# A narrow expert's gate in another order, and two raw weight slots turned into halves of split weights

## The chip, the cores and the metric

The kernel runs on one NeuronCore of a Trainium2 chip. TensorE (PE in the profile) multiplies, with weight loads (PEld) running beside the matmuls; VectorE (DVE) and ScalarE (ACT) do elementwise work; GpSimd (POOL) has a little of it in the dense layers; SyncE (SP) issues the loads from HBM. The metric is the device time of one execution in microseconds. The median of three runs of the kernel before is 1550.54 us (1549.85 to 1551.14). One more execution was profiled: it took 1551.01 us, of which 1549.3 us lie between its first and its last instruction.

## The reference, cut to what matters

Two encoder layers on 256 tokens of width 1024, all in float32. What the change touches is the end of the second layer, an expert block that takes most of the time:

```python
def swiglu(xn, w_gu, w_down):
    g, u = jnp.split(xn @ w_gu, 2, axis=-1)
    return (jax.nn.silu(g) * u) @ w_down

def moe_swiglu(xn, router, w_gu, w_down):     # 8 experts of hidden width 3584, each token to 2 of them
    ...
    for e in range(N_EXPERTS):
        out = out + comb[..., e:e + 1] * swiglu(xn, w_gu[e], w_down[e])
    return out
```

Ahead of it come a gated convolution and pooling mixer, two cross-attentions, a dense SwiGLU and a Conformer convolution, with the same kind of weights.

## The kernel before, in words

**Split weights.** TensorE takes its operands in a reduced float32 form (`fp32r`). So that the result keeps float32's precision, each operand is split into two parts: `hi`, a cast of the value, and `lo`, the value less `hi`. A weight chunk is 128 partitions x 2048 float32 (1 MB). `load` (line 143) brings it into a slot of the pool `rawp`, or in the expert block also into one of six `spare` tiles. `split` (line 152) makes its parts in two halves of 1024 columns: for each half a cast on ACT (line 168), and behind it a subtraction on DVE (line 169). The halves lie in the pools `hip` and `lop`, `NPART` slots each. With `NPART = 4` the parts of two chunks exist at a time. A raw slot is free again when its last subtraction is done; a slot of the parts, when TensorE is done with it.

**The expert block** goes through eight positions (`expert`, line 1112), each an expert with the tokens that chose it. In a position j runs over seven strips of 512 hidden columns. A strip has six chunks: two for the gate (`gate_up(j, 0)`), two for the up projection (`gate_up(j, 1)`), two for the down projection of the strip before (`down`). Positions 0, 1, 3, 5 and 7 are wide: up to 128 tokens, three products to a weight (line 211, 212 and 216), twelve matmuls to a chunk. Positions 2, 4 and 6 are narrow: at most 64 tokens. There the tokens' `hi` and `lo` parts stand side by side as 128 columns, so that a chunk takes eight matmuls (line 1108), and PSUM holds the `hi` tokens' results in partitions 0 to 63 and the `lo` tokens' in 64 to 127. The last up chunk of a narrow strip is not split but multiplied as plain float32 (line 1124).

**The gate of a narrow strip** (`gate`, line 1137) runs when both products of the strip are issued. ACT copies the two 64-partition halves of the gate's PSUM tile crosswise into an SBUF tile `esg` (lines 1141 and 1142), DVE adds the PSUM tile to it on 128 partitions (line 1143), so that the sum stands in both halves, and ACT takes the silu (line 1144). DVE then multiplies with the up product into `eh` (line 1148). `to_rows` turns `eh` with TensorE (line 1157) and splits the result on ACT and DVE (lines 1038 and 1039) for the down products.

**The order of the work.** Each engine executes its instructions in one fixed order. In the expert block that order is found by a planner while the kernel is built: it follows the order of the program as a priority and takes what its own model of the engines holds to be ready. `tc.issue_after(x)` makes the instructions of a block come behind `x` where they are on the same engine. SP's loads in the expert block stand in program order; `NAHEAD` of them are issued in the attention ahead of it. `RING` and `kinds` say which load takes a raw slot and which a spare tile, with a period of `NRAW + 6`.

**Raw slots outside the expert block.** In the dense layers all weights pass through the same `NRAW = 11` slots. From the end of the dense SwiGLU to the Conformer's end, six of them hold three pairs of parts split early (`raw_pair`), and one more holds a half of a key weight (`apart`). In the Conformer the weights `pw1` are multiplied unsplit (`product_whole`, line 255), so each holds its raw slot until its product is done.

Of the kernel before, what the change touches and what calls it, by code (L numbers as in the profile page):

```python
# [25 lines left out]
F32 = mybir.dt.float32  # L26
F32R = mybir.dt.float32r
I32 = mybir.dt.int32
AF = mybir.ActivationFunctionType
# [3 lines left out]
P = 128  # L33
# [16 lines left out]
HALF = CAP // 2  # L50
TCKW = dict(schedule_with_timeline_sim=True)
NCKW = dict(dynamic_dma_scratch_size=512)
NRAW = 11
NPART = 4
RING = "rrrrrrrrsssssrrrrrs"
P2_POOL = (0, 2, 4, 6)
NWARM = 10
NAHEAD = 13
G_TAPS = 4 * (11, 12)


# [20 lines left out]
def _build(ctx, tc, io, cap):  # L82
    nc = tc.nc
    PSUM = bass.MemoryType.PSUM
    const = ctx.enter_context(tc.tile_pool(name="const", bufs=1))
    rawp = ctx.enter_context(tc.tile_pool(name="rawp", bufs=NRAW))
    hip = ctx.enter_context(tc.tile_pool(name="hip", bufs=NPART))
    lop = ctx.enter_context(tc.tile_pool(name="lop", bufs=NPART))
    big = ctx.enter_context(tc.tile_pool(name="big", bufs=10))
    work = ctx.enter_context(tc.tile_pool(name="work", bufs=2))  # L90
    w2b, w1b = 4, 5
# [6 lines left out]
    V, S, G, PE = nc.vector, nc.scalar, nc.gpsimd, nc.tensor  # L98

    def f32(ap):  # L100
        return ap.bitcast(F32)
# [4 lines left out]
    def acc_tile(name="acc"):  # L106
        return psA.tile([P, 512], F32, tag="acc", name=name)
# [4 lines left out]
    def tr_tile(name="tr", dt=F32):  # L112
        return psT.tile([P, 512], dt, tag="tr", name=name)
# [29 lines left out]
    def load(ap, n=CH, pieces=1, spare=False):  # L143
        raw = big_tile("spare") if spare else rawp.tile([P, CH], F32, tag="raw", name="raw")
        for i in range(pieces):
            sl = slice(i * n // pieces, (i + 1) * n // pieces)
            nc.sync.dma_start(raw[:, sl], ap[:, sl])
        return raw

    done = []  # L150
# [535 lines left out]
    half = KF // 2  # L686
    ps = None
    for m in range(KD):
# [6 lines left out]
        for hf in range(2):  # L695
# [4 lines left out]
            for kk in range(half):  # L700
                k = hf * half + kk
                h, sl = hid[k // 8], slice((k % 8) * T, (k % 8 + 1) * T)
# [218 lines left out]
    ahead = deque()  # L921
    kinds = list(RING)

    def fetch():
        n, (ap, pieces) = next(source)
        ahead.append(load(ap, pieces=pieces, spare=kinds[n] == "s"))
        kinds.append(kinds[-(NRAW + 6)])

    for _ in range(NAHEAD):
        fetch()  # L930
# [103 lines left out]
    def side_by_side(dst, src):  # L1034

        v = dst.rearrange("p (k s n) -> p k s n", s=2, n=HALF)
        src = src.rearrange("p (k n) -> p k n", n=HALF)
        S.copy(v[:, :, 0, :], src)
        V.tensor_sub(v[:, :, 1, :], src, f32(v[:, :, 0, :]))
# [48 lines left out]
    def out_tiles():  # L1088
        return [psE.tile([P, 512], F32, tag="py", name=f"py{n}") for n in range(2)]
# [5 lines left out]
    def whole_chunk():  # L1095
        if not ahead:
            fetch()
        return ahead.popleft()

    def chunk(pieces=2):  # L1100
        return split(whole_chunk(), pieces=pieces)

    def narrow(ps, xs, ws, first, last):

        n = len(xs)
        for part in range(2):
            for i, (x, w) in enumerate(zip(xs, ws)):
                ins = PE.matmul(ps, x, w[part], start=first and i == part == 0,  # L1108
                                stop=last and part == 1 and i == n - 1)
        return ins  # L1110

    def expert(e, g, following):
        nonlocal fn
        py = out_tiles()
        two = e in NARROW

        def gate_up(j, gu):
            pz = acc_tile("gu")
            for kh in range(2):
                xs = [xg[:, k * P:(k + 1) * P] for k in range(kh * 4, kh * 4 + 4)]  # L1120
                if two and gu == kh == 1:
                    w = whole_chunk()
                    for kk in range(4):
                        PE.matmul(pz, f32(xs[kk]), w[:, kk * 512:(kk + 1) * 512],  # L1124
                                  start=False, stop=kk == 3)
                    continue
                w = chunk()
                ws = [w(kk * 512, (kk + 1) * 512) for kk in range(4)]
                if two:
                    narrow(pz, xs, ws, kh == 0, kh == 1)  # L1130
                    continue
                moving(pz, [(xg[:, k * P:(k + 1) * P], xg[:, D + k * P:D + (k + 1) * P])
                            for k in range(kh * 4, kh * 4 + 4)],
                       ws, kh == 0, kh == 1)
            return pz

        def gate(pg, pu):
            sg = work.tile([P, 512], F32, tag="w2", name="esg", bufs=w2b)
            if two:

                S.copy(sg[:HALF], pg[HALF:])
                S.copy(sg[HALF:], pg[:HALF])
                V.tensor_add(sg, sg, pg)
                S.activation(sg, sg, AF.Silu, scale=g.cw[:, 1:2])
            else:
                S.activation(sg, pg, AF.Silu, scale=g.cw[:, 1:2])
            h = work.tile([P, 512], F32, tag="w2", name="eh", bufs=w2b)
            V.scalar_tensor_tensor(h, pu, g.cw[:, 1:2], sg, op0=ALU.mult, op1=ALU.mult)
            return h

        def to_rows(j, h):
            pt = tr_tile("ht")
            o = (j % 2) * D
            if two:

                for i in range(4):
                    PE.matmul(pt[:, i * HALF:(i + 1) * HALF], h[:, i * P:(i + 1) * P], both,
                              start=True, stop=True)
                return side_by_side(ht[:, o:o + 512], pt[:, :4 * HALF])
            for i in range(4):  # L1160
                PE.transpose(pt[:, i * P:(i + 1) * P], h[:, i * P:(i + 1) * P], ident)
            S.copy(ht[:, o:o + 512], pt)
            V.tensor_sub(ht[:, o + 512:o + D], pt, f32(ht[:, o:o + 512]))

        def down(j, n):
            w = chunk(4 if e == NE - 1 and j == 6 else 2)
            o = (j % 2) * D
            if two:
                return narrow(py[n], [ht[:, o + f * P:o + (f + 1) * P] for f in range(4)],
                              [w(f * 512, (f + 1) * 512) for f in range(4)], j == 0, j == 6)  # L1170
            return moving(py[n],
                   [(ht[:, o + f * P:o + (f + 1) * P], ht[:, o + 512 + f * P:o + 512 + (f + 1) * P])
                    for f in range(4)],
                   [w(f * 512, (f + 1) * 512) for f in range(4)], j == 0, j == 6)

        def weighted(n):
            src = py[n]
            hi, lo = (work.tile([P, 512], F32R, tag="w2", name=name, bufs=w2b) for name in ("yh", "yl"))
            S.activation(hi, src, AF.Copy, scale=g.cw[:, 0:1])
            done[:] = [V.scalar_tensor_tensor(lo, src, g.cw[:, 0:1], f32(hi),  # L1180
                                              op0=ALU.mult, op1=ALU.subtract)]
            return hi, lo

        def scatter(n, y, tile=tr_tile):
            for t in range(2):
                pz = tile("so")
                PE.matmul(pz, g.oT[:, t * P:(t + 1) * P], y[0], start=True, stop=False)
                PE.matmul(pz, g.oT[:, t * P:(t + 1) * P], y[1], start=False, stop=True)
                a = acc[:, t * D + n * 512:t * D + (n + 1) * 512]
                V.tensor_add(a, a, pz)  # L1190

        h = None
        for j in range(7):
            pg = gate_up(j, 0)
            if j:
                to_rows(j - 1, h)
            pu = gate_up(j, 1)
            h = gate(pg, pu)
            if j:
                down(j - 1, 0)  # L1200
                if j == 6:
                    to_rows(6, h)
                down(j - 1, 1)
            if following is not None and j in (3, 5):
                following.step(j)
        if following is not None:
            following.rows()
        else:
            fn = big_tile("fn")
            nc.sync.dma_start(fn[:, :D], io["final_norm"].to_broadcast([P, D]))  # L1210
        down(6, 0)
        y = weighted(0)
        last = down(6, 1)
        if following is not None:
            scatter(0, y)
            scatter(1, weighted(1))
        else:
            y1 = weighted(1)
            with tc.issue_after(last.ins):
                scatter(0, y)  # L1220
            scatter(1, y1, acc_tile)

    g = Gather(0)
# [88 lines left out]
    for e in range(NE):  # L1312
        following = Gather(e + 1) if e + 1 < NE else None
        expert(e, g, following)
        g = following
# [174 lines left out]
```

## Time and profile before

| | us |
|---|---|
| median of three runs | 1550.54 |
| the profiled execution | 1551.01 |
| its span, first to last instruction | 1549.3 |
| expert block, first gate matmul to the last down matmul | 594.1 to 1533.5 |
| one strip of a wide position | 16.8 |
| one strip of a narrow position | 13.0 to 15.6 |

Busy time of an engine is the union of its instructions. The end of a matmul is modelled, and matmuls overlap in the pipeline, so PE can look busy where the next matmul comes late; weight loads show the pace as well. An idle stretch of an engine carries the name of what ended it. The profile's share of DMA is the mean busy share of the 16 DMA engines.

### The profile page before, as it was taken

The numbers are of one execution on the slowest core, as the hardware profiler recorded it, in microseconds if no ns is written. First come the engines' busy times: TensorE is split into PE (matmuls) and PEld (weight loads), VectorE is DVE, ScalarE is ACT, GpSimd is POOL, SyncE is SP. The second block draws the span as 40 slices with busy tenths as digits, with TensorE's granted clock in tenths as the row PEclk, the third lists the DMA queues.
The fourth block names the chain that finished last, engine by engine and source line by source line (L and its number), as shares of the span: only waits on it lengthen the run. The fifth ranks groups of instructions, "written<-read, shape, count | busy, mean of one in ns | idle before, by whom it ended". The sixth has DMA issues, their size and how long they took to land.

```text
span 1549.3 us, 23644 instructions
## 1 busy us (share of the span) xinstructions
PE 1513.3 (98%) x8558; PEld 1295.2 (84%) x8558; DVE 1298.1 (84%) x1730; ACT 1052.1 (68%) x1381; POOL 149.0 (10%) x230
## 2 busy tenths in 40 slices
PE   8899999999999999999999999999999999999996
PEld 8899999999998998888888778888667888667885
DVE  7866677776898868989989989889889888889897
ACT  6454554455575657777777877777777777777775
POOL 4710000001294210000000000000000000000000
PEclk9999999999999999999999999999999999999998
DMA  9654454436545566999999999999999999999940
GB/s 371 266 181 159 146 176 166 138 98 226 210 137 222 186 254 217 378 370 335 373 374 336 402 422 407 382 364 341 406 395 378 370 362 341 403 398 371 387 177 30
DMA packets 65214, 451.43 MB, mean 291 GB/s; under 512 B 7360, under 2 KB 7488, under 8 KB 12480
## 3 DMA queue, kind: packets, MB, share of 16 engines
q1 hardware_dynamic: 65088, 449.83, 76.7%
q8 instruction: 69, 1.13, 0.3%
q14 instruction: 57, 0.47, 0.1%
HBM read 448.75 MB, written 1.05 MB: 290 GB/s over the span
## 4 chain that ended last, share of the span: by engine, by line
PE 81%; DVE 9%; POOL 3%; issue 3%; ACT 2%; DMA 1%; SPq 0%; DVEq 0%; POOLq 0%; ACTq 0%
PE gu L211 8%; PE gu L212 8%; PE gu L216 8%; PE acc L205 7%; PE acc L204 7%; PE acc L203 7%; DVE lo L169 7%; PE gu L1124 5%; PE gu L1108 4%; PE py L211 4%; PE py L216 4%; PE py L212 4%; PE py L1108 3%; POOL part L764 2%; PE gx L1027 1%
## 5 line engine op out<-in xcount | busy, mean ns | idle before, releaser
L169 DVE TENSOR_TENSOR lo<-raw,hi 128x1024 fp32r<-128x1024 f32 (+3 forms) x573 | 671.0, 1208 | 120.1 <-ACT hi L168 110.4
L168 ACT CAST hi<-raw 128x1024 fp32r<-128x1024 f32 (+3 forms) x573 | 565.6, 1031 | 213.5 <-PE acc L204 92.0
L169 DVE TENSOR_TENSOR lo<-spare,hi 128x1024 fp32r<-128x1024 f32 (+1 forms) x226 | 261.4, 1203 | 24.6 <-ACT hi L168 20.5
L168 ACT CAST hi<-spare 128x1024 fp32r<-128x1024 f32 (+1 forms) x226 | 221.5, 1036 | 23.6 <-PE gu L212 11.9
L211 PE MATMUL gu<-hi,xg 128*128 128x512 f32 x560 | 218.8, 391 | 0.0
L212 PE MATMUL gu<-hi,xg 128*128 128x512 f32 x560 | 218.4, 390 | 0.0
L216 PE MATMUL gu<-lo,xg 128*128 128x512 f32 x560 | 154.2, 391 | 0.7 <-DVE lo L169 0.7
L216 PEld LDWEIGHTS gu<-lo,xg 128*128 128x128 f32 x560 | 104.7, 188 | 23.9 <-DVE lo L169 1.9
L211 PEld LDWEIGHTS gu<-hi,xg 128*128 128x128 f32 x560 | 105.1, 188 | 22.2 <-ACT hi L168 0.2
L212 PEld LDWEIGHTS gu<-hi,xg 128*128 128x128 f32 x560 | 105.1, 188 | 21.8
L211 PE MATMUL py<-hi,ht 128*128 128x512 f32 x280 | 111.1, 398 | 0.0
L212 PE MATMUL py<-hi,ht 128*128 128x512 f32 x280 | 109.3, 390 | 0.0
L205 PE MATMUL acc<-a2h,lo 128*128 128x256 f32 x336 | 95.2, 283 | 0.0
L204 PE MATMUL acc<-a2l,hi 128*128 128x256 f32 x336 | 95.2, 283 | 0.0
L203 PE MATMUL acc<-a2h,hi 128*128 128x256 f32 x336 | 95.1, 283 | 0.0
L1386 POOL TENSOR_TENSOR fo<-accum,fn 128x512 f32<-128x512 f32 x2 | 2.5, 1268 | 949.1 <-DVE accum L1190 949.1
L1108 PE MATMUL gu<-lo,xg 128*128 128x512 f32 x252 | 80.3, 411 | 8.0 <-DVE lo L169 8.0
L216 PE MATMUL py<-lo,ht 128*128 128x512 f32 x280 | 84.0, 395 | 0.0
L1108 PE MATMUL gu<-hi,xg 128*128 128x512 f32 x252 | 71.2, 396 | 0.0
L1108 PEld LDWEIGHTS gu<-lo,xg 128*128 128x128 f32 x252 | 43.4, 188 | 31.6 <-DVE lo L169 25.2
L203 PEld LDWEIGHTS acc<-a2h,hi 128*128 128x128 f32 x336 | 64.5, 192 | 0.0
L205 PEld LDWEIGHTS acc<-a2h,lo 128*128 128x128 f32 x336 | 64.5, 192 | 0.0
(421 smaller groups left out, 3176.9 us busy)
## 6 DMA issues: line engine op xcount, KB each, us to landing
raw<-in_moe_gu SPq DMA_DIRECT2D x139, 1024.0 KB, 7.1
spare<-in_moe_gu SPq DMA_DIRECT2D x85, 1024.0 KB, 7.2
raw<-in_moe_down SPq DMA_DIRECT2D x78, 1024.0 KB, 7.3
spare<-in_moe_down SPq DMA_DIRECT2D x32, 1024.0 KB, 7.0
raw<-in_ffn_gu SPq DMA_DIRECT2D x22, 1024.0 KB, 4.8
raw<-in_pw SPq DMA_DIRECT2D x12, 1024.0 KB, 4.9
raw<-in_ffn_down SPq DMA_DIRECT2D x16, 704.0 KB, 4.1
raw<-in_wk SPq DMA_DIRECT2D x8, 1024.0 KB, 7.1
```

What stands on the lines that cost most here:

```text
L168: done[:] = (S.copy(hi[:, i:i + step], raw[:, a + i:a + i + step]), V.tensor_sub(lo[:, i:i + step], raw[:, a + i:a + i + step], f32(hi[:, ...
L169: V.tensor_sub(lo[:, i:i + step], raw[:, a + i:a + i + step], f32(hi[:, i:i + step])))
L203: PE.matmul(ps, a[0], b[0], start=first, stop=False)
L204: PE.matmul(ps, a[0], b[1], start=False, stop=False)
L205: PE.matmul(ps, a[1], b[0], start=False, stop=last)
L211: PE.matmul(ps, a[0], b[0], start=first and i == 0, stop=False)
L212: PE.matmul(ps, a[1], b[0], start=False, stop=False)
L216: ins = PE.matmul(ps, a[0], b[1], start=False, stop=last and i == n - 1)
L764: G.tensor_add(part, part, prod)
L1027: PE.matmul(px[:, kk * P:(kk + 1) * P], xt[:, t * D + d0:t * D + d0 + P], oh[:, t, :], start=t == 0, stop=t == 1)
L1108: ins = PE.matmul(ps, x, w[part], start=first and i == part == 0, stop=last and part == 1 and i == n - 1)
L1124: PE.matmul(pz, f32(xs[kk]), w[:, kk * 512:(kk + 1) * 512], start=False, stop=kk == 3)
```

## The change

The pools: `NRAW` goes from 11 to 9, `NPART` from 4 to 6, in the same SBUF space; `RING` and `NAHEAD` follow the shorter ring. The gate in narrow positions: one copy instead of two, the addition on 64 partitions, both written in the program right behind the gate's products, ahead of `to_rows` and the up products. The silu is taken twice from the 64-partition sum, first into the upper half and then in place, and these instructions come behind the last cast on ACT of the up products (`done[0]`). In wide positions the gate stays as it is.

```diff
-NRAW = 11
-NPART = 4
-RING = "rrrrrrrrsssssrrrrrs"
+NRAW = 9
+NPART = 6
+RING = "rrrrrrrsssssrrrrs"
...
-NAHEAD = 13
+NAHEAD = 12
...
-        def gate(pg, pu):
-            sg = work.tile([P, 512], F32, tag="w2", name="esg", bufs=w2b)
+        def gate(pg, pu, sg):
             if two:
 
-                S.copy(sg[:HALF], pg[HALF:])
-                S.copy(sg[HALF:], pg[:HALF])
-                V.tensor_add(sg, sg, pg)
-                S.activation(sg, sg, AF.Silu, scale=g.cw[:, 1:2])
+                for half in (sg[HALF:], sg[:HALF]):
+                    S.activation(half, sg[:HALF], AF.Silu, scale=g.cw[:HALF, 1:2])
             else:
+                sg = work.tile([P, 512], F32, tag="w2", name="esg", bufs=w2b)
                 S.activation(sg, pg, AF.Silu, scale=g.cw[:, 1:2])
...
             pg = gate_up(j, 0)
+            sg = None
+            if two:
+                sg = work.tile([P, 512], F32, tag="w2", name="esg", bufs=w2b)
+                S.copy(sg[:HALF], pg[HALF:])
+                V.tensor_add(sg[:HALF], sg[:HALF], pg[:HALF])
             if j:
                 to_rows(j - 1, h)
             pu = gate_up(j, 1)
-            h = gate(pg, pu)
+            with tc.issue_after(done[0].ins) if two else nullcontext():
+                h = gate(pg, pu, sg)
```

## Rows read from the trace of the kernel before

**Rows 1.** The page's busy times: us, share of the span, instructions.

```profile
PE 1513.3 (98%) x8558; PEld 1295.2 (84%) x8558; DVE 1298.1 (84%) x1730; ACT 1052.1 (68%) x1381; POOL 149.0 (10%) x230
```

**Rows 2.** Stretches of narrow positions 2, 4, 6: length, busy times, PEclk, DMA share, GB/s.

```profile
838.00:940.00 102.00, 101.15 (x439) 74.39 (x437) 93.83 (x97) 84.37 (x102) 0.00 (x0) 1.00 0.98 395
1063.00:1177.00 114.00, 109.85 (x454) 76.04 (x454) 98.14 (x105) 85.26 (x104) 0.00 (x0) 1.00 0.97 384
1300.00:1412.00 112.00, 107.85 (x447) 74.42 (x446) 96.88 (x100) 83.76 (x103) 0.00 (x0) 1.00 0.98 383
```

**Rows 3.** The same view cut at starts of the narrow gate's product; last row wide.

```profile
862.64:916.55 53.91, 53.91 (x229) 39.81 (x228) 49.29 (x51) 46.67 (x56) 0.00 (x0) 1.00 1.00 416
890.13:903.09 12.96, 12.96 (x55) 9.53 (x54) 12.96 (x13) 10.99 (x13) 0.00 (x0) 1.00 1.01 424
916.55:932.11 15.56, 14.71 (x57) 9.54 (x56) 13.12 (x14) 12.01 (x16) 0.00 (x0) 1.00 1.01 422
1088.93:1167.07 78.14, 73.99 (x287) 48.35 (x286) 65.77 (x67) 59.20 (x73) 0.00 (x0) 1.00 1.00 401
1323.86:1402.00 78.14, 73.99 (x287) 48.36 (x286) 65.77 (x66) 59.21 (x73) 0.00 (x0) 1.00 1.00 401
1002.17:1018.96 16.79, 16.79 (x77) 13.91 (x76) 15.06 (x14) 12.65 (x15) 0.00 (x0) 1.00 0.98 375
```

**Rows 4.** The chain that ended last, in a stretch of position 4, by line.

```profile
by line: DVE lo L169 48.3%; PE gu L1124 23.5%; issue 17.4%; PE gu L1108 4.5%; PE py L1108 4.2%; DVE ht L1039 2.5%; DVEq L169 0.6%; DVE eh L1148 0.2%; PE ht L1157 0.2%
```

**Rows 5.** Timeline of ACT in position 4: start, length, instruction, idle before it.

```profile
1122.55 5.79 ACT L168 CAST hi<-raw 128x1024 fp32r<-128x1024 f32 x6
1129.91 0.59 ACT L1141 COPY esg<-gu 64x512 f32<-64x512 f32 x1 [1.57 <-PE gu L1108]
...
1131.99 0.72 ACT L1144 ACTIVATE esg<-esg,cw 128x512 f32<-128x512 f32 x1 [0.90 <-DVE esg L1143]
1132.62 1.98 ACT L168 CAST hi<-raw 128x1024 fp32r<-128x1024 f32 x2
```

**Rows 6.** Timeline of DVE in the same strip.

```profile
1131.27 0.69 DVE L1143 TENSOR_TENSOR esg<-esg,gu 128x512 f32<-128x512 f32 x1
1133.68 1.23 DVE L169 TENSOR_TENSOR lo<-raw,hi 128x1024 fp32r<-128x1024 f32 x1 [1.72 <-ACT hi L168]
1135.63 0.75 DVE L1148 SCALAR_TENSOR_TENSOR eh<-gu,cw,esg 128x512 f32<-128x512 f32 x1 [0.72 <-PE gu L1124]
```

**Rows 7.** Timeline of all engines in a strip of position 2.

```profile
898.69 0.58 ACT L1142 COPY esg<-gu 64x512 f32<-64x512 f32 x1
899.25 3.59 PE L1124 MATMUL gu<-raw,xg 128*128 128x512 f32 x8
899.29 1.99 ACT L168 CAST hi<-spare 128x1024 fp32r<-128x1024 f32 x2
900.23 0.68 DVE L1143 TENSOR_TENSOR esg<-esg,gu 128x512 f32<-128x512 f32 x1
900.82 2.36 DVE L169 TENSOR_TENSOR lo<-spare,hi 128x1024 fp32r<-128x1024 f32 x2
901.19 0.72 ACT L1144 ACTIVATE esg<-esg,cw 128x512 f32<-128x512 f32 x1
```

**Rows 8.** Costliest groups of ACT, shapes apart: busy us, mean ns, idle before.

```profile
L1162 ACT CAST ht<-ht 128x512 fp32r<-128x512 f32 x35 | 20.5, 584 | 34.4 <-PE ht L1161 34.4
```

**Rows 9.** SP's timeline in position 4: its last four loads.

```profile
1124.24 7.48 SPq L147 DMA_DIRECT2D raw<-in_moe_down  x4
```

**Rows 10.** SP's waits, 360 to 520 us: us in total, times, longest.

```profile
SPq L147 <- PE acc L255: 45.1, 8, 6.9
```

**Rows 11.** Loads by destination: count, size, median us from issue to landing.

```profile
raw<-in_moe_down SPq DMA_DIRECT2D x78, 1024.0 KB, 7.3
raw<-in_pw SPq DMA_DIRECT2D x12, 1024.0 KB, 4.9
```

**Rows 12.** Timeline of PE in the Conformer: one product of an unsplit weight.

```profile
434.20 7.07 PE L255 MATMUL acc<-a,raw 128*128 128x256 f32 x32
```

## The prediction

> **What bounds the kernel now.** I read the page's busy times first. PE is busy 98% of the span, DVE 84%, ACT 68% [rows 1]: by these the kernel is TensorE's, and little is left. The change aims at the three narrow positions, so the next view is busy time by stretch. In positions 2, 4 and 6 PE sits idle 0.85, 4.15 and 4.15 us [rows 2], 9.15 us together (102.00 less 101.15, and so on).
>
> That is not the whole loss. Cut into strips, from one `eh` to the next, a narrow strip takes 12.96 us at best, with PE and DVE both busy throughout. Four strips of position 2 take 53.91 us, 13.48 each. The last strip of position 2 takes 15.56, and the five whole strips in each of positions 4 and 6 take 78.14, 15.63 each [rows 3]. The work is the same: PEld is busy 9.53 us in the 12.96 us strip and 48.35/5 = 9.67 in the slow ones. So the slow strips lose about 2.7 us, of which the matmuls' busy time shows 0.8 (78.14 less 73.99, over 5).
>
> By the Trainium skill ("Perfetto Trace Analysis", Identifying the Most-Contended Engine) matmul busy time is a poor measure of the room left, because matmuls are pipelined, and weight-load time a better one. By the first measure the change could win 9 us at most; by the second some 30 (2.7 in 11 strips), and the equal weight loads in strips of 13 and 15.6 us bear the second out.
>
> Where do the 2.7 us go? The chain through position 4 is 48% subtractions and 24% the plain float32 chunk [rows 4], so they alternate. The timelines show how. ACT casts the up halves, waits 1.57 us for the gate's products, copies twice, waits 0.90 us for DVE's addition, takes the silu, and only then casts for the down chunk, at 1132.62 [rows 5]: 1129.91 + 0.59 + 0.58 + 0.90 + 0.72 with small overlaps. DVE, done with the addition at 1131.96, has nothing to subtract until 1133.68. It gets one half in, and then `eh`, next in its queue, waits 0.72 us for the float32 chunk's end [rows 6]. DVE thus idles 2.44 us beside PE's chunk, and afterwards PE waits for DVE. In position 2 the plan has two casts between copies and silu, two subtractions before `eh`, and no such hole [rows 7]. A slow strip is an order of the queues, not a lack of an engine: DVE works 13.1 us in either kind [rows 3].
>
> **The change part by part.**
>
> *Two part slots more each (4 to 6).* ACT may be three chunks ahead of PE instead of two. At the gate's copies the slots hold the second gate chunk and the up chunk; now the down chunk fits beside them. ACT's 1.57 us wait can be two casts (1.98 us the pair [rows 5]), and DVE then has two subtractions (2.36 us [rows 7]) to do in the 1.72 us in which it had none. By itself this fills the hole if the planner uses it.
>
> *Copy and addition behind the gate's products, silu behind the last up cast.* ACT has one copy (0.59) fewer and one silu more. A silu on 64 partitions has no row. From below it is the 64-partition copy, 0.58; from above the 128-partition silu, 0.72 [rows 5, 7]. I take 0.72, since a 64-partition copy of 512 columns takes as long as a 128-partition cast of 512 (0.59 against 584 ns [rows 5, 8]): partitions don't count. The addition on 64 partitions stays at 0.69 for the same reason (halved, 0.34, at best). So ACT gains 0 to 0.14 us a strip, 2.9 us in 21 strips at most. What hides it is ACT's free time: 59.20/5 = 11.84 us of work in a strip of 13.5 [rows 3]; without that cover it is 2.9 us. The copies' wait for the gate's products remains; queued behind it on ACT are casts, for which DVE waits, and behind those PE. That is the danger of the earlier place, priced among the rivals. The gate's PSUM tile comes free earlier and `esg` is held longer (one of four slots); neither is waited for in these rows, so 0, to either side a us or two at the three position changes.
>
> *Two raw slots fewer (ring 17 to 15), one load fewer ahead.* In position 4 SP issues the last four loads from 1124.24, in 7.48 us; 7.3 us later the last has landed, at about 1139 [rows 9, 11]. TensorE needs those chunks after the last `eh` at 1167.07 [rows 3], 28 us later; at 2.6 us a chunk (15.6 over 6) some 10 chunks wait landed. With 15 slots 8 or 9 wait. A strip of 13.5 us wants six chunks, 6.29 MB, or 466 GB/s, and the best stretch gave 424 [rows 3]: 14.8 us, so 1.3 us a strip and 9 us a position, or 3.5 chunks, come out of the stock. A wide strip of 16.79 us gives back 2 us. The stock lasts; cost 0. If the cover were gone, narrow strips would take 14.8.
>
> *The same slots in the dense layers.* Six raw slots hold early parts and one `apart`; 9 - 7 = 2 are left for `pw1`, where there were 4. SP already waits for these products, 45.1 us in eight waits [rows 10], harmlessly, since loads run ahead. With two slots a load is issued as a product ends, and its 4.9 us [rows 11] fit beside the next product's 7.07 [rows 12]: cost 0. More part slots let casts run ahead in the dense layers too; PE is fed there, 0, bounded by a few us either way.
>
> The Trainium skill (the same page, Optimization Strategy) takes a gap that repeats for a sign of too few buffers. By that rule the four part slots alone are at fault and the gate's edit is idle. Position 2 differs: its fast strips ran with the same four. The sum is the same by either, since both are changed.
>
> **The sum.** All slow strips go to the mean of position 2's fast four, 13.5 us. Positions 4 and 6: 78.14 - 67.5 = 10.64 each, 21.3. The last strip of position 2: 15.56 - 13.5 = 2.1. Together 23.4, against the profiled execution's 1551.0 (span 1549.3 and 1.7 around it): 1527.6. The three runs' median, 1550.5, is half a us lower, so I say 1527.5. At best, all strips at 12.96: (78.14 - 64.8) x 2 + (69.47 - 64.8) = 31.4, or 1519.6; a few us at the position changes could come on top. What is late next is DVE: 13.1 us of work in a strip of 13.5, so no more is to be had without taking work from it.
>
> **Rivals.**
>
> *Half of it.* The planner keeps one of the two holes: the silu again directly behind the addition, as [rows 5] show, or `eh` too early [rows 6]. For it: order alone made 13 or 15.6 in this trace, and the planner is the same. Against: six slots allow ACT and DVE to work ahead. A strip of 14.5: 78.14 - 72.5 = 5.6 twice, and 1: 12.3, so 1538.5.
>
> *No gain.* The copy, now ahead of the up casts in the program, stands ahead of them on ACT and waits for the gate's end with casts behind it. Copy 0.59, addition 0.69, subtraction 1.2 then pass before PE's first up `lo`, where four `hi` matmuls cover about 1 us (12.96 us over 55 of them [rows 3], 0.24 each): 1.5 us, and more for the second half. The hole has only moved: strips stay near 15.6, 1550.5. Against: with more slots the up casts can be done before the gate's products are. It decides by whether casts of the up chunk stand before the copy.
>
> *Slower: the Conformer starves.* If a third long-held raw tile leaves `pw1` one slot, each of six products waits for its load: 6 x 4.9 = 29 us, against the 23 won: 1557. For it: SP waits for these products already. Against: the count leaves two, and 4.9 is under 7.07. It decides from the point where one slot is left between two products.
>
> **How the numbers follow.** The forecast 56% (its own range 1516 to 1536), half of it 17%, no gain 13%, slower 12%, and 2% a time below 1516, won at the position changes or in the dense layers besides. 1514 to 1552 leaves out the slower case and a sliver. About 0.2%, 3.1 us, is what a measurement of this kernel can tell from no change. Forecast, half and the rest below it make 0.75 faster; of no gain most is the same, 0.11; slower 0.14, with the part of no gain that comes out above.
>
> **What would show it.** Strips from `eh` to `eh` in positions 4 and 6 of 13.0 to 14, like position 2's; DVE's 1.72 us wait for a cast behind the addition gone, casts between addition and silu; the chain there mostly subtractions, no longer alternating with the float32 chunk; wide strips still 16.8; products of line 255 still 7 us apart. Wrong would be: strips at 15.6 with ACT waiting for the gate's products ahead of up casts, PE idle behind `pw1` loads, or narrow strips of 14.8 with DMA at its limit.

## The result and the profile after

The changed kernel takes 1563.5 us (median of 4 runs, 1561.7 to 1564.0), where the kernel before takes 1550.5 (1549.9 to 1551.1). The ratio is 1.0082, 95% interval 1.0065 to 1.0099: slower by 0.8%. The forecast was 1527.5, faster, and the range ended at 1552. It was wrong in sign.

The profiled execution took 1561.7 us, its span 1560.0, 10.7 more than before. First the page's busy times, to be held against [rows 1].

```profile
PE 1518.6 (97%) x8558; PEld 1294.1 (83%) x8558; DVE 1298.2 (83%) x1730; ACT 1049.7 (67%) x1381; POOL 151.1 (10%) x230
```

The number of instructions is the same, and so, within 3 us, is the work of DVE and ACT; the kernel waits more. Next, stretches from `eh` to `eh` (length, then busy PE, PEld, DVE, ACT, POOL, granted clock, DMA share, GB/s): five strips of position 2, its first and its last, a wide strip, five strips of positions 4 and 6.

```profile
868.67:942.43 73.76, 71.41 (x287) 48.87 (x286) 60.84 (x64) 56.03 (x69) 0.00 (x0) 1.00 1.00 416
868.67:881.97 13.30, 13.30 (x58) 9.79 (x57) 11.44 (x14) 10.78 (x15) 0.00 (x0) 1.00 0.97 407
926.87:942.43 15.56, 14.70 (x57) 9.53 (x56) 13.09 (x15) 11.89 (x15) 0.00 (x0) 1.00 1.00 411
1012.48:1029.27 16.79, 16.79 (x77) 13.90 (x76) 15.06 (x14) 12.65 (x15) 0.00 (x0) 1.00 0.97 368
1099.33:1177.40 78.07, 73.95 (x287) 48.33 (x286) 65.56 (x67) 59.62 (x72) 0.00 (x0) 1.00 0.99 400
1334.70:1412.80 78.10, 73.75 (x286) 47.99 (x285) 65.59 (x68) 59.64 (x72) 0.00 (x0) 1.00 0.99 397
```

Positions 4 and 6 stand where they stood: 78.07 and 78.10 us against 78.14 [rows 3]. Nothing of the forecast's gain came. Position 2 got slower: its strips are 13.3, 14.2, 14.8, 15.9 and 15.6 us, where they were 14.0, 13.4, 13.0, 13.5 and 15.6. That is 4.3 us of the 10.7. Before it, the first `eh` of the expert block starts at 614.0, not 608.5: 5.5 us come from the dense layers. The rest, 0.9 us, is what gains and losses in the wide positions and at the changes between positions leave.

**A narrow strip after.** ACT in position 4, to be read against [rows 5] (start, length, instruction, idle before it and what ended it):

```profile
1132.90 3.90 ACT L168 CAST hi<-spare 128x1024 fp32r<-128x1024 f32 x4
1136.69 2.00 ACT L168 CAST hi<-raw 128x1024 fp32r<-128x1024 f32 x2
1140.26 0.58 ACT L1196 COPY esg<-gu 64x512 f32<-64x512 f32 x1 [1.57 <-PE gu L1108]
1142.34 1.47 ACT L1141 ACTIVATE esg<-esg,cw 64x512 f32<-64x512 f32 x2 [1.50 <-DVE esg L1197]
1143.72 3.87 ACT L168 CAST hi<-raw 128x1024 fp32r<-128x1024 f32 x4
```

DVE beside it, against [rows 6]:

```profile
1139.36 2.35 DVE L169 TENSOR_TENSOR lo<-raw,hi 128x1024 fp32r<-128x1024 f32 x2
1141.63 0.67 DVE L1197 TENSOR_TENSOR esg<-esg,gu 64x512 f32<-64x512 f32 x1
1144.77 1.23 DVE L169 TENSOR_TENSOR lo<-raw,hi 128x1024 fp32r<-128x1024 f32 x1 [2.47 <-ACT hi L168]
1145.97 0.75 DVE L1146 SCALAR_TENSOR_TENSOR eh<-gu,cw,esg 128x512 f32<-128x512 f32 x1
```

ACT still casts six halves and then waits 1.57 us at the copy, though there are six part slots. DVE's hole behind the addition was 1.72 us, and `eh` then waited 0.72: together 2.44. Now the hole is 2.47 and `eh` waits for nothing. It is the two silus, 1.47, and one cast, 1.0, in a row: ACT may not cast for the down chunk until the silus are done, and they wait for an addition that stands on DVE behind the up chunk's subtractions. DVE's 13.1 us of work and 2.47 are the strip of 15.6. The waits in those five strips say it too (us in total, times, longest); before, the first of these lines had 8.6, 5, 1.7 and the silu's wait for the addition 4.5, 5, 0.9:

```profile
DVE lo L169 <- ACT hi L168: 14.9, 6, 2.5
ACT esg L1141 <- DVE esg L1197: 7.4, 5, 1.5
```

**The dense layers.** SP's loads around the Conformer, in the kernel before:

```profile
387.28 0.33 SPq L147 DMA_DIRECT2D raw<-in_wv  x1
391.24 0.33 SPq L147 DMA_DIRECT2D raw<-in_wk  x1
405.75 2.76 SPq L147 DMA_DIRECT2D raw<-in_pw  x3
```

and after:

```profile
400.58 0.33 SPq L147 DMA_DIRECT2D raw<-in_wv  x1
404.00 0.33 SPq L147 DMA_DIRECT2D raw<-in_wk  x1
410.91 3.15 SPq L147 DMA_DIRECT2D raw<-in_pw  x2
```

Product 0 of `pw1` ends at 403.8. Its slot goes at 404.00 to the fourth `wk` chunk, and the third product's load (product 2) must wait for product 1's slot, free at 410.91. With 4.9 us of flight it lands at 415.8, where product 2 begins; before, product 2 began at 413.0 although everything ahead of it was 2.3 us later then. PE's timeline after shows the wait, with products 2, 3 and 4 behind it:

```profile
415.76 23.49 PE L255 MATMUL acc<-a,raw 128*128 128x256 f32 x96 [4.88 <-DMA raw<-in_pw]
```

The wait is not the whole cost. These are product 2 before, and then, after, a part of product 2, all of it, and product 3 (columns as above):

```profile
413.05:419.95 6.90, 6.90 (x33) 6.08 (x32) 6.47 (x17) 5.14 (x12) 5.20 (x8) 1.00 0.68 262
```

```profile
416.60:419.50 2.90, 2.90 (x8) 2.27 (x8) 2.90 (x9) 0.51 (x1) 2.59 (x5) 0.50 0.41 170
415.76:425.27 9.51, 9.51 (x33) 7.98 (x33) 9.51 (x25) 1.19 (x3) 4.49 (x7) 0.73 0.21 87
425.27:432.18 6.91, 6.91 (x34) 6.08 (x33) 6.55 (x17) 5.66 (x13) 5.16 (x8) 1.00 0.46 152
```

While PE waits, its granted clock falls to 0.50, the lower of its two levels (1.2 GHz against 2.4), and product 2 takes 9.51 us instead of 6.90. So the late load costs 4.9 us of waiting and 2.6 us of slower matmuls. Less the 2.3 us by which this execution was ahead (0.5 us in `raw9_only` below), that is the 5.3 us by which product 3 starts late, and nearly all of the expert block's 5.5.

### The profile page after: what moved, and what is told of

The parts are those of the page before. It is cut to its first block, busy times and chain, and to the rows that moved or that the text cites. A ratio compares the mean times of both kernels' runs of the same rounds, so it can differ in the third digit from the quotient of the medians.

```text
span 1560.0 us, 23466 instructions
## 1 busy us (share of the span) xinstructions
PE 1518.6 (97%) x8558; PEld 1294.1 (83%) x8558; DVE 1298.2 (83%) x1730; ACT 1049.7 (67%) x1381; POOL 151.1 (10%) x230
## 4 chain that ended last, share of the span: by engine, by line
PE 75%; DVE 13%; issue 5%; ACT 3%; POOL 2%; DMA 1%; SPq 0%; DVEq 0%; POOLq 0%; ACTq 0%
DVE lo L169 8%; PE gu L216 8%; PE gu L211 8%; PE gu L212 8%; PE acc L204 7%; PE acc L205 7%; PE acc L203 7%; PE py L211 4%; PE py L216 4%; PE py L212 4%; PE gu L1124 2%; PE gu L1108 2%; PE py L1108 2%; DVE cacc L770 2%; PE acc L255 2%
## 5 line engine op out<-in xcount | busy, mean ns | idle before, releaser
L169 DVE TENSOR_TENSOR lo<-raw,hi 128x1024 fp32r<-128x1024 f32 (+3 forms) x557 | 645.2, 1196 | 109.9 <-ACT hi L168 102.8
L168 ACT CAST hi<-raw 128x1024 fp32r<-128x1024 f32 (+3 forms) x557 | 542.9, 1024 | 194.2 <-PE acc L204 77.5
L169 DVE TENSOR_TENSOR lo<-spare,hi 128x1024 fp32r<-128x1024 f32 x242 | 283.5, 1219 | 38.8 <-ACT hi L168 36.6
L168 ACT CAST hi<-spare 128x1024 fp32r<-128x1024 f32 x242 | 238.7, 1049 | 24.8 <-PE gu L212 15.9
L216 PE MATMUL py<-lo,ht 128*128 128x512 f32 x280 | 79.8, 391 | 0.0
L764 POOL TENSOR_TENSOR part<-part,prod 128x256 f32<-128x256 f32 x84 | 61.1, 743 | 47.7 <-ACT prod L763 43.6
```

What stands on the lines that cost most here:

```text
L168: done[:] = (S.copy(hi[:, i:i + step], raw[:, a + i:a + i + step]), V.tensor_sub(lo[:, i:i + step], raw[:, a + i:a + i + step], f32(hi[:, ...
L169: V.tensor_sub(lo[:, i:i + step], raw[:, a + i:a + i + step], f32(hi[:, i:i + step])))
L216: ins = PE.matmul(ps, a[0], b[1], start=False, stop=last and i == n - 1)
L764: G.tensor_add(part, part, prod)
```

## The experiments

Each ratio is to the kernel before (medians 1550.3 to 1550.6).

**The two parts of the change, each alone.** `gate_only` has the new gate and the old pools (`NRAW = 11`, `NPART = 4`, old `RING`, `NAHEAD = 13`); `pools_only` has the new pools and the old gate.

> Only the gate's edit, with the pools of before (11 raw slots, 4 part slots, ring 17, 13 loads ahead). Theory: the time lost comes from the pools and the narrow strips are set by the order of the queues, which the gate's edit leaves as it was (silu directly behind the addition, casts for the down chunk behind the silu). So third pw1 product at 413 us +-1 as before, strips of positions 4 and 6 still 15.5 to 15.7, position 2 from first to last eh 77 to 80 us as before: 1549 to 1553 us. Rival, the gate's edit itself costs: 1556 us or more, with position 2 at 81 us or longer.

> Only the pools' edit (9 raw slots, 6 part slots, ring 15, 12 loads ahead), with the gate of before. Theory: it has the whole loss. Third pw1 product waits some 5 us for its load (start near 415 instead of 413, the fourth 5 us late), position 2 is 3 to 5 us longer because its order settles earlier into the slow one, positions 4 and 6 stay at 15.6 a strip though six part slots are there: 1559 to 1565 us. Rival, six part slots help and the new gate spoils it: strips of 13 to 14.5 us and 1540 us or less.

Measured: `gate_only` 1551.5, ratio 1.0006 (0.9996 to 1.0015): nothing. `pools_only` 1562.7, ratio 1.0075 (1.0059 to 1.0092): the whole loss, with the third product at 417.5 instead of near 415. Position 4 shows that neither part shortens a strip (five strips of `gate_only`, then of `pools_only`):

```profile
1088.80:1166.90 78.10, 73.96 (x287) 48.31 (x286) 65.56 (x67) 59.65 (x72) 0.00 (x0) 1.00 1.00 400
```

```profile
1101.20:1179.40 78.20, 74.14 (x289) 48.40 (x288) 65.85 (x67) 59.27 (x73) 0.00 (x0) 1.00 1.00 401
```

**Fewer raw slots, or more part slots?** `raw9_only` is the kernel before with nine raw slots and four part slots.

```diff
-NRAW = 11
+NRAW = 9
-RING = "rrrrrrrrsssssrrrrrs"
+RING = "rrrrrrrsssssrrrrs"
-NAHEAD = 13
+NAHEAD = 12
```

> The kernel before with nine raw slots, ring 15 and 12 loads ahead, part slots still four, old gate: the two slots' memory stays unused. Theory (raw slots alone make the dense loss and position 2's): third pw1 product 4 to 6 us late, position 2 from first to last eh 79 to 82 us, strips of 4 and 6 at 15.6: 1556 to 1563 us. Rival (six part slots let casts run ahead on ACT and DVE and delay the dense layers): 1549 to 1553 us.

Measured: 1560.8, ratio 1.0067 (1.005 to 1.0084). The first `eh` starts at 614.9, 6.4 late; position 2's five strips take 72.4 us against 69.5 and turn slow one strip earlier than before; positions 4 and 6 are unchanged. Taking two raw slots away, with the ring and the loads ahead that follow from it, is the loss, and two part slots more give nothing for it.

**The silu behind the down chunk's casts.** In narrow strips the first down chunk is split ahead of the gate's end, so that `done[0]` is its last cast and not the up chunk's. `late_after` does this to the changed kernel, `late_gate_only` to `gate_only`. `chunk()` splits the next chunk of the load order; `down` takes it as `wd`.

```diff
...
+            wd = chunk() if two and j else None
             with tc.issue_after(done[0].ins) if two else nullcontext():
                 h = gate(pg, pu, sg)
...
-                down(j - 1, 0)
+                down(j - 1, 0, wd)
```

> The changed kernel, with one edit: in narrow positions the first down chunk is split ahead of the gate's second half, so that the silu stands behind the casts of that chunk instead of behind those of the up chunk. Theory: the narrow strip is a loop of DVE (13.1 us), silu (1.5) and one cast (1.0), and it opens when two casts stand between copy and silu: strips of 13.0 to 13.8 us in positions 4 and 6, DVE's wait of 2.47 us gone, 10 us less in each of the two and 3 to 5 less in position 2; the Conformer's loss stays: 1536 to 1543 us. Rival, something else holds the strip at 15.6 (loads, or PE's chain through the plain float32 chunk): 1558 to 1564 us.

> The same edit (silu behind the casts of the first down chunk) and the changed gate, but with the pools of before. Theory: four part slots are enough, as in position 2 of before: strips of 13.0 to 13.8 in positions 4 and 6, no loss in the Conformer: 1526 to 1533 us. Rival, four part slots are too few, since the down chunk's casts must wait for the slots of the second gate chunk: strips of 14.5 to 15.6 and 1540 to 1552 us.

Measured: 1556.5 (ratio 1.0039, 1.0024 to 1.0053) and 1545.6 (0.9965, 0.9953 to 0.9978). They gain 7.0 us on the changed kernel and 5.9 on `gate_only`, at most a third of what was expected: strips fell to 15.2, not to 13.5. For `late_gate_only` that lies in its rival's range (four part slots too few), but with six part slots `late_after` has the same strips, so the slots are not what holds them. In `late_gate_only` DVE's hole behind the addition is gone, and a new wait stands at `eh`:

```profile
1129.18 0.67 DVE L1197 TENSOR_TENSOR esg<-esg,gu 64x512 f32<-64x512 f32 x1
1129.78 2.35 DVE L169 TENSOR_TENSOR lo<-raw,hi 128x1024 fp32r<-128x1024 f32 x2
1133.59 0.75 DVE L1146 SCALAR_TENSOR_TENSOR eh<-gu,cw,esg 128x512 f32<-128x512 f32 x1 [1.47 <-PE gu L1124]
```

`eh` waits for the up product's float32 chunk on PE, and behind it stand the second down chunk's subtractions, which PE wants next. The loop was the order of two queues, and one of the two had been mended.

**`eh` behind the second down chunk's subtractions too.** `eh_behind_before_pools` has four part slots and eleven raw ones, `eh_behind_six_parts` six and nine. `product_of` is the last line of the old `gate`, the product `eh`; `done[1]` is the last subtraction on DVE.

```diff
...
-            wd = chunk() if two and j else None
+            wd, we = (chunk() if two and j else None), None
             with tc.issue_after(done[0].ins) if two else nullcontext():
-                h = gate(pg, pu, sg)
+                sg = gate(pg, pu, sg)
+            if two and j:
+                we = chunk()
+            with tc.issue_after(done[1].ins) if two else nullcontext():
+                h = product_of(pu, sg)
...
-                down(j - 1, 1)
+                down(j - 1, 1, we)
```

> As late_gate_only (pools of before, changed gate, silu behind the casts of the first down chunk), and besides the second down chunk is split ahead of the gate's product eh, which stands behind that chunk's last subtraction on DVE. What is left in late_gate_only's strip of 15.2 us is DVE's wait of 1.5 us at eh for the float32 chunk, and 0.5 for a cast behind the turned rows. Theory (the strip is a loop through DVE's queue; four subtractions instead of two fit beside the float32 chunk): strips of 13.0 to 14.0 in positions 4 and 6, 8 us less in each of the two, 1526 to 1534 us. Rival (four part slots bind: the second down chunk's casts wait for the slots of the up chunk and all later ones come late): strips of 14.5 or more, 1540 us or more.

> The same edit on the changed kernel's pools (9 raw, 6 part slots). Theory: strips of 13.0 to 13.8, and position 2 too, where four slots keep a mixed order; Conformer's loss of 5 to 7 us and position 1 to 2 stay: 1533 to 1541 us. Rival (the strips' 15 us come from elsewhere): 1553 us or more.

Measured: 1531.9 (ratio 0.988, 0.9863 to 0.9896), which beats both kernels, and 1540.9 (0.994, 0.9923 to 0.9956). In position 4 the strips are 13.5, 14.1, 13.5, 14.7 and 14.3 us with four part slots, and the same with six. The five together, first `eh_behind_before_pools`, then `eh_behind_six_parts`:

```profile
1089.05:1159.17 70.12, 69.02 (x288) 49.81 (x287) 65.42 (x68) 59.94 (x72) 0.00 (x0) 1.00 1.01 418
```

```profile
1096.60:1166.80 70.20, 69.08 (x288) 49.88 (x287) 65.52 (x68) 59.73 (x72) 0.00 (x0) 1.00 1.01 417
```

So the strip was an order, as the prediction read it, and two part slots more have no part in it. The Trainium skill ("Perfetto Trace Analysis", Optimization Strategy) says that a repeating gap can mean too few buffers; here six part slots left it at 15.6 us, and the order alone closed most of it with four.

**Which part of the gate's edit is needed?** `whole_gate_moved` is `eh_behind_before_pools` with the gate's old arithmetic in the new place: two copies, the addition and one silu on 128 partitions.

```diff
                 S.copy(sg[:HALF], pg[HALF:])
-                V.tensor_add(sg[:HALF], sg[:HALF], pg[:HALF])
+                S.copy(sg[HALF:], pg[:HALF])
+                V.tensor_add(sg, sg, pg)
...
-                for half in (sg[HALF:], sg[:HALF]):
-                    S.activation(half, sg[:HALF], AF.Silu, scale=g.cw[:HALF, 1:2])
+                S.activation(sg, sg, AF.Silu, scale=g.cw[:, 1:2])
```

> Like eh_behind_before_pools (1531.9 us: eleven raw slots, four part slots, silu behind the first down chunk's casts, eh behind the second's subtractions), but with the gate of before the change: both halves copied, the addition and the silu on 128 partitions, each once. Copies and addition stand behind the gate's products, as there. If the places of silu and eh are the whole gain, strips in positions 4 and 6 stay at 13.5 to 14.7 us and the time is 1530 to 1535. Rival: the halved gate (one copy fewer ahead of the addition, one silu more behind it) carries a part; then the second copy, 0.58 us between the gate's end and the addition, lengthens each strip, some 0.5 us in 17 strips, and the time is 1538 to 1542.

Measured: 1544.9 (ratio 0.9965, 0.9953 to 0.9978), 13 us slower than with the halved gate. That is beyond even the rival's range, and a copy of 0.58 us in 17 strips can't make it. ACT's timeline in a strip of 15.2 us shows another order:

```profile
1122.33 0.37 ACT L1038 CAST ht<-ht 128x256 fp32r<-128x256 f32 x1 [2.51 <-PE ht L1157]
1122.60 3.89 ACT L168 CAST hi<-raw 128x1024 fp32r<-128x1024 f32 x4
1126.88 0.58 ACT L1198 COPY esg<-gu 64x512 f32<-64x512 f32 x1 [0.39 <-PE gu L1108]
```

in place of, in `eh_behind_before_pools`:

```profile
1119.60 0.37 ACT L1038 CAST ht<-ht 128x256 fp32r<-128x256 f32 x1 [0.55 <-PE ht L1158]
1119.87 2.00 ACT L168 CAST hi<-raw 128x1024 fp32r<-128x1024 f32 x2
1122.88 0.59 ACT L1199 COPY esg<-gu 64x512 f32<-64x512 f32 x1 [1.01 <-PE gu L1108]
```

With the other gate the planner puts `ht`'s cast two casts earlier, and ACT waits 2.51 us there with four casts behind. `whole_gate_rows_later` takes that choice from it:

```diff
             pg = gate_up(j, 0)
-            sg = None
+            sg, mark = None, done[0]
...
             if j:
-                to_rows(j - 1, h)
+                with tc.issue_after(mark.ins) if two else nullcontext():
+                    to_rows(j - 1, h)
```

> whole_gate_moved (1544.9 us; strips 15.2) with one edit: in narrow strips the rows of h (ht: its products, cast and subtraction) come on ACT and DVE behind the last cast and subtraction of the gate's second chunk, as the planner had them by itself in eh_behind_before_pools, where whole_gate_moved had them one chunk earlier and ACT waited 2.51 us for ht's products. If only that order made the 13 us between the two, ACT's 2.51 us wait goes, strips fall to 13.5 to 14.7 us, and the time is 1530 to 1536 with the gate of before. Rival: the second copy and the addition on 128 partitions cost by themselves; then the order is mended and strips stay above 14.5, 1540 to 1545.

Measured: 1532.5 (ratio 0.9882, 0.9865 to 0.9898), strips of 13.5, 14.0, 13.5, 15.4 and 14.3 us. ACT's wait at `ht` is as short as with the halved gate:

```profile
1118.95 0.37 ACT L1038 CAST ht<-ht 128x256 fp32r<-128x256 f32 x1 [0.59 <-PE ht L1157]
```

The old gate's instructions and the old pools, in another order, give what the best version gives. By these medians the halved gate is worth 0.7 us, less than can be told.

**What the raw slots cost in the dense layers.** All three start from `eh_behind_six_parts`. `no_apart` gives the fourth `wk` chunk's second half no tile of its own. `third_product_early` loads three `pw1` chunks ahead of `wk`'s last two. `ten_and_five` has ten raw and five part slots.

```diff
-        k1.append(split(load(io["wk"][1, 3]), apart=(1,)))
+        k1.append(split(load(io["wk"][1, 3])))
```

```diff
-    pw1 = [load(io["pw1"][c]) for c in range(2)]
+    pw1 = [load(io["pw1"][c]) for c in range(3)]
...
-        ps = product_whole(pw1[c] if c < 2 else load(io["pw1"][c]), whole_of(a3))
+        ps = product_whole(pw1[c] if c < 3 else load(io["pw1"][c]), whole_of(a3))
```

```diff
-NRAW = 9
-NPART = 6
-RING = "rrrrrrrsssssrrrrs"
+NRAW = 10
+NPART = 5
+RING = "rrrrrrrrsssssrrrrs"
```

> The previous kernel without the key weight's half in a raw slot (with six part slots it can lie there), so the Conformer has three raw slots for pw1 where the changed kernel had two. Theory (the third pw1 product waits because pairs, apart, the raw key chunk and the running product hold all nine slots): the third product waits 0 to 2 us instead of 4.9, Conformer's loss 0 to 3 us instead of 7.6: 4 to 7 us less than the previous kernel, 1527 to 1536 us. Rival (the wait comes from loads issued later by the planner, whatever the slots): no change against the previous kernel.

> eh_behind_six_parts (nine raw slots, 1540.9 us) with one edit in the Conformer: the third pw1 product's load stands with the first two, ahead of the loads of wk's third and fourth chunk, so it doesn't wait for the slot that these hold. If the raw slots cost the dense layers by that one late load, the 4.9 us wait at the third product goes and the expert block begins 4 to 6 us earlier: 1535 to 1537. Rival, as no_apart suggests: with nine slots another load is late in its place (wk's third chunk, or the fourth product's); then the expert block begins at most 2 us earlier and the time is 1539 to 1543.

> eh_behind_six_parts with ten raw slots and five part slots in place of nine and six, in the same space; the ring and the loads ahead follow (period 16, 12 ahead). If one raw slot was lacking in the Conformer, its third product no longer waits, the strips are as with four and six parts (13.5 to 14.7 us), and the time is 1532 to 1535, near the 1531.9 of eleven and four. Rival: the loss goes slot by slot, half of it stays: 1536 to 1539.

Measured: `no_apart` 1540.2 (ratio 0.9934, 0.9918 to 0.9951), a miss. The third product's wait shrinks from 4.9 to 3.0 us, and the first seven products take 2.6 us less, but the first `eh` starts at 615.1, no earlier than the 614.4 of `eh_behind_six_parts`. What the products gained is lost again behind them, in part where the clock is at 0.50 once more, from 566.4; where the rest goes stays open. The `apart` tile's slot alone is not enough.

`third_product_early` 1553.0 (1.0017, 1.0007 to 1.0027), a miss on the far side. Product 2 starts at 410.6, on time, but the loads behind it are late: `wk`'s chunks, for which ACT and DVE wait (us in total, times, longest, from 380 to 470 us), and product 3's own load, as SP's and PE's timelines show. The first `eh` starts at 626.8.

```profile
DVE lo L169 <- ACT hi L168: 16.2, 2, 12.0
ACT hi L168 <- DMA raw<-in_wk: 9.7, 3, 4.3
```

```profile
419.62 4.26 SPq L147 DMA_DIRECT2D raw<-in_pw  x2
424.73 15.45 PE L255 MATMUL acc<-a,raw 128*128 128x256 f32 x64 [7.07 <-ACT prod L763]
```

PE's wait of 7.07 us ahead of product 3 stands under an instruction of ACT, but it ends as the load issued at 419.62 lands, 4.9 us later by [rows 11]. The granted clock falls to 0.50 in that wait and three more times before the expert block.

With nine slots some load is late in any order tried. `ten_and_five` 1534.3 (0.9894, 0.9878 to 0.9911): held. The third product's load is issued at product 0's end again, and PE waits for none of the eight products:

```profile
401.80 0.33 SPq L147 DMA_DIRECT2D raw<-in_wk  x1
405.57 14.14 SPq L147 DMA_DIRECT2D raw<-in_pw  x4
```

`ten_and_five` also issues 12 loads ahead, as the nine-slot kernels do, so that number is not the cause. The loss is a step, not a slope: the tenth slot is the one that counts, and the first `eh` is back at 609.5.

## Why the prediction was wrong

Between forecast and result lie 36.0 us. Of these 23.4 are the gain that did not come, 5.5 the dense layers, 4.3 position 2, and 0.9 the rest of the expert block; 1.8 is how far the profiled execution lies below the median.

**What was right.** That a slow strip is an order of ACT's and DVE's queues, with the work unchanged: three kernels with that order mended take 70.1 to 70.6 us for the five strips that took 78.1, with the same 65 to 66 us on DVE. That weight loads are the better measure of the room and matmul busy time a poor one, as the Trainium skill has it ("Perfetto Trace Analysis", Identifying the Most-Contended Engine): PE was busy in 73.99 of 78.14 us [rows 3], a room of 4, and 8 were won; weight loads were busy in 48.35. That the halved instructions cost as much as whole ones: two silus 1.47, the addition 0.67 against 0.69. That wide strips stay at 16.8 and that the stock of landed chunks lasts: no engine waits for a load in positions 4 and 6, not even in `eh_behind_six_parts`, with 15 slots and strips of 14.0.

**"By itself this fills the hole if the planner uses it."** This step failed. The "if" carried 56% and was not looked into: [rows 5] show six casts and then a wait at the copy, and what stands behind a copy in a fixed queue can't fill the wait ahead of it, however many slots are free. `pools_only` has the six slots and strips of 15.6.

**"Silu behind the last up cast."** In [rows 5] the silu stood behind the last up cast already. The edit named a place that it had; what had to move was the down chunk's casts, ahead of it, and then `eh` and `ht`. With this the term of 23.4 us in the sum is 0 for the change, and 18.0 to 18.5 for the order it aimed at. The target was too low as well: DVE does not work "13.1 us in either kind", but 12.3 on average in the four fast strips (49.29 over four [rows 3]), which thus were fast with less work; with 13.1 of it the mended strips take 14.0 on average, not 13.5. The rival "no gain" had the strips' outcome and not the mechanism: it had the copy ahead of the up casts, and the copy stayed behind them.

**"With two slots a load is issued as a product ends ... cost 0."** This step failed too. The count left out the fourth `wk` chunk's own raw tile, loaded between `pw1`'s second and third. It takes product 0's slot, as SP's rows show, and the third load comes a whole product late: 4.9 us of waiting, and 2.6 more because the clock falls meanwhile, which no step of the prediction had. This is the mechanism of the slower rival, which had the price of one wait right, 4.9 us, and its number wrong: it comes once and not six times. That the rival's 1557 lies nearest to the result is luck: it set 29 us of waits against a gain of 23, and neither came.

**Position 2.** The prediction took its fast strips for given. They are the start of a run that settles into the slow order after some strips, and with nine raw slots it settles earlier: `raw9_only` loses 2.9 us there, `pools_only` and the changed kernel 4.3. No rival had this. Why the planner settles earlier stays open. It is not a late load on the chip: no engine waits for a load in position 2 of either kernel.

## What to carry to other kernels

Where an engine's queue is fixed, read a repeating hole as an order: write down which instruction stands at the head of each queue when the hole opens, what is behind it, and whether the edit changes that very sequence; more slots and smaller instructions did not here. Mend all the queues of the loop, since the first move only shows the next wait (15.6, 15.2, 13.5 to 14.7 us here). Before a ring of buffers is shortened, count every tile that is held at its tightest moment in load order, the one just being loaded included. And price a wait of TensorE with what follows it: here 4.9 us of waiting brought 2.6 us of slower matmuls.

## What the runs showed of the hardware that was not expected

A wait of TensorE cost more than its length. In the five kernels that have nine raw slots and load the Conformer's weights as before (the changed kernel, `pools_only`, `raw9_only`, `late_after`, `eh_behind_six_parts`) the granted clock is 0.50 from 416.6 to 419.5, behind a wait of some 5 us. In the kernels with ten and eleven, in which PE does not wait there, it is 1.00 in that stretch, and product 2 takes 6.9 us instead of 9.3 to 9.6.

The five strips of 70.1 us moved 418 GB/s, 29.3 MB, where they used 31.5 MB (five times 6.29): the difference came from chunks landed in the wide position before. So strips of 14.0 us ran below the 14.8 that the best measured rate of 424 GB/s would allow alone [rows 3], with the DMA engines busy throughout.
